# Two transformer blocks on one core: relative bias read back skewed from DRAM, and three re-orderings in the first mixer

## The chip, the cores and the metric

The kernel runs on one core of one Trainium2 chip. The metric is the device time of one execution, in microseconds. Before the change it is 933.23 us, the median of 3 runs (931.76 to 933.48).

## The reference, cut to what matters

The program computes two transformer blocks, one after the other, on 256 tokens of width 1024 in float32. Each block is a token mixer followed by a mixture of 32 experts. The change is in the mixer of the first block, and there in the attention branch:

```python
qb = rms_norm(qb.reshape(b, t, 8, 64), g_q)
kb = rms_norm(kb.reshape(b, t, 8, 64), g_k)
score = einsum('bqhs,bqh->bqs', relu(q_idx . k_idx), w_idx)   # indexer, then the top 64 keys of each query
logits = einsum('bqhd,bqkhd->bqhk', qb, k_sel) * 64 ** -0.5
bias = rel_bias[t5_bucket(key_pos - query_pos)]               # (32, 8) table, one number per head and distance
p = softmax(logits + bias)
out = einsum('bqhk,bqkhd->bqhd', p, v_sel)
```

The bias depends on the head and on key minus query position alone, so 512 numbers per head hold all of it. A tile of 128 queries needs, in partition p, the row of those numbers shifted by p: later queries see smaller distances.

## The kernel before, in words

**Weights** stream from DRAM through 5 slots of 2 MB; a load into a slot is issued from SP's queue as soon as the weight that stood there has been used up. The order of loads in the first mixer is index, keys (KB), queries (QB), values (VB), then the projections of the gated linear attention (GLA_R, GLA_QK, GLA_V), the gates, the branch and output matrices, and then the experts.

**A projection** (`project`, L314) multiplies the 256 tokens by a 1024x512 weight in 8 steps of k. For each step `split` (L268) cuts the 128x512 weight piece into two parts that TensorE takes in its fast float32r form: ACT copies the rounded value (`whi`, L279) and DVE or POOL subtracts it from the weight (`wlo`, L280). Which of the two subtracts follows from the string in `SPLIT_ENGINES` that `turn[2]` selects: 'vp' alternates between DVE and POOL. There are 4 buffers of `whi` and of `wlo`. A step is six 512-column matmuls (L285) for the two token tiles.

**The order of work.** The instructions are written in one program, and a planner in the library fixes each engine's queue when the kernel is built. It walks the program with its own cost estimates and gives an engine, at each point, the ready instruction that stands first in the program; a split is moved ahead by 30 places (`SPLIT_AHEAD`). It also gives out the buffers of a tag. The queues run in that fixed order on the chip, so an instruction that waits holds up everything behind it on its engine.

**The attention branch** of the first mixer, in program order: the index projection and its scores (L524 to L541, DVE's multiply-adds at L557 and L559, the eight rounds of MAX8 and MATCH_REPLACE8 at L564 and L565, and the mask at L567); the key projection and its norm `kn` (L570; `head_norm`, L361, with the squares at L367, the sums at L368 and the multiply at L371); the bias row; the query projection; `pairs_T` of the keys (L374: 8 transposes at L381, two evictions on DVE at L387); the norm of the queries and their `pairs_T`; the value projection; then `scores` (L409) per tile of 128 queries: the mask matmuls (L596), the score matmuls (L422), the addition of the bias on DVE (`add_rel`, L599), maximum, exponentials and `values`.

**The bias row.** A matmul of the bias table with a one-hot bucket table (L573) gives 8 heads x 512 distances; DVE copies it to `relT` (L574), a tile of the tag "sq", of which there are 2 buffers (`head_norm` uses the same tag for its squares). SP writes it to DRAM as 8 rows of 2 KB (`rel_d`, L575) and, when that has landed, reads it back twice (L578): partition p reads the 256 numbers from place p on, so rows run the wrong way round. Four groups of matmuls with an anti-diagonal matrix, `flip` (L587), turn the 128 partitions upside down, and ACT copies the result into `relB` (L589).

**Loads at the start**: SP issues the first half of `X` (L223), then the pack `zk` with the identity matrix (L216), then the second half of `X`. The first instructions of TensorE transpose `X` (L348) and need both.

Of the kernel before, what the change touches and what calls it, by code (L numbers as in the profile page):

```python
# [11 lines left out]
F32 = mybir.dt.float32  # L12
# [3 lines left out]
AF = mybir.ActivationFunctionType  # L16
# [4 lines left out]
P = 128  # L21
T = 256
NT = 2
# [3 lines left out]
CAP = 32  # L27
N_STREAM = 5
SPLIT_AHEAD = 30
SPLIT_ENGINES = ('vp', 'pv')  # L30
LAST_COLUMNS = ((0, 2), (2, 1), (3, 1))
WCOLS = 4096

# [1 line left out]
QB, KB, VB, IDX, GATE_A, GATE_B = 1552, 2064, 2576, 3088, 3384, 4408  # L35
# [36 lines left out]
def tables(a):  # L72
    z, c, m1, m2, e = (Pack() for _ in range(5))
    i = np.arange(P)
    f = np.float32

    def feat(name, shape=(8, P)):
        return a[name].reshape(shape).T

    def twice(name):  # L80
        return np.concatenate([a[name].reshape(64, 1)] * 2, 0)

    z.add("ident", np.eye(P, dtype=f))
    z.add("g_mix", feat("g_mix"))

    c.add("g_ffn", feat("g_ffn"))
    c.add("g_ffn_i", a["g_ffn"].reshape(P, 8))
    c.add("ggla", a["g_gla"].reshape(P, 1))
    c.add("n_mix", feat("norm_mix_2"))
    c.add("n_ffn", feat("norm_ffn_2"))  # L90
    c.add("n_ffn_i", a["norm_ffn_2"].reshape(P, 8))
    c.add("br1", rows(np.concatenate([a["b_rg"].ravel(), a["b_re"].ravel()])))
    c.add("br2", rows(np.concatenate([a["b_router_group_2"].ravel(), a["b_router_expert_2"].ravel()])))
    c.add("iota", rows(np.arange(CAP, dtype=f) - 4096))
    c.add("rev4", rows(f(4) - np.arange(4, dtype=f)))
    c.add("owner", ((i[:, None] // 32) == np.arange(4)[None, :]).astype(f))

    m1.add("gq", twice("g_q"))
    m1.add("gk", twice("g_k"))
    m1.add("wa2", np.concatenate([a["w_alpha2"].reshape(16, 256), a["b_alpha"].reshape(1, 256)], 0))  # L100
    m1.add("relb", a["rel_bias"].reshape(32, 8))
    same = (i[:, None] // 64) == (i[None, :] // 64)
    m1.add("after", ((i[:, None] > i[None, :]) & same).astype(f) / 16)
    m1.add("chunk", ((i[:, None] // 64) == np.arange(2)[None, :]).astype(f) / 16)
    m1.add("flip", np.eye(P, dtype=f)[::-1])

    m2.add("gqf", twice("q_norm_fox_2"))
    m2.add("gkf", twice("k_norm_fox_2"))
    c.add("gof", feat("out_norm_fox_2", (4, P)))
    m2.add("god", feat("out_norm_dil_2", (4, P)))  # L110
    m2.add("gqd", rows(a["q_norm_dil_2"]))
    m2.add("gkd", rows(a["k_norm_dil_2"]))
    m2.add("bfg", rows(a["b_forget_2"]))
    m2.add("upto", (i[:, None] <= i[None, :]).astype(f))
    inv = (f(1) / (f(10000.0) ** (np.arange(0, 64, 2, dtype=f) / f(64)))).astype(f)
    ang = np.arange(T, dtype=f)[:, None] * inv[None, :]
    for name, fn in (("cos", np.cos), ("sin", np.sin)):
        m2.add(name, fn(ang).astype(f).reshape(2, P, 32).transpose(1, 0, 2).reshape(P, 64))
    m2.add("selrow", (((i[:, None] % 32) == np.arange(8)[None, :]) & (i[:, None] < 96)).astype(f))
    d = i[:, None] + P - np.arange(T)[None, :]  # L120
    n = ((d >= 0) & (d <= 128)).astype(int) + ((d >= 0) & (d % 4 == 0)) + ((d >= 0) & (d % 16 == 0))
    m2.add("ln", np.where(n > 0, np.log(np.maximum(n, 1)), NEG).astype(f))

    rel = np.arange(512) - 255
    e.add("bucket", (t5_bucket(rel)[None, :] == np.arange(32)[:, None]).astype(f))
    e.add("before", (i[:, None] < i[None, :]).astype(f))
    e.add("causal", np.where(i[None, :] > i[:, None], f(NEG), f(0)).astype(f))
    return {"zk": z, "ck": c, "m1": m1, "m2": m2, "ek": e}
# [25 lines left out]
def two_blocks(ctx: ExitStack, tc: tile.TileContext, A: dict, at: dict, out: bass.AP):  # L154
    nc = tc.nc
# [39 lines left out]
    def bank(name="ps", bufs=4):  # L195
        return psum.tile([P, 512], F32, name=name, tag=name, bufs=bufs)
# [11 lines left out]
    def t5(shape, dt=F32):  # L208
        return wtile(shape, dt, tag="b5", bufs=2, level="misc")

    X = const.tile([P, NT, D], F32, name="X")
    packs = {}

    def load_pack(name, level="const"):
        packs[name] = wtile([P, A[name].shape[1]], tag=name, bufs=1, level=level)
        nc.sync.dma_start(packs[name], A[name])  # L216

    def con(name):
        p, o, n = at[name]
        return packs[p][:, o:o + n]  # L220

    for tt in range(NT):
        nc.sync.dma_start(X[:, tt, :], A["x"][0, tt * P:(tt + 1) * P, :])  # L223
        if tt == 0:
            load_pack("zk")

    open_phase("mix1")
    open_phase("mix1_b4", "mid")
# [37 lines left out]
    turn = [0, None, 0]  # L266
# [47 lines left out]
    def project(src, c0, ns, hT, then=None, step=8):  # L314
        ws = [wload(src, 8 * (c0 + sum(ns[:i])), 8, n, step) for i, n in enumerate(ns)]
        ac = [[acc() for _ in range(NT)] for _ in ns]
        gemm_tok(ws, hT, ac, then)
        return ac if len(ns) > 1 else ac[0]
# [42 lines left out]
    def head_norm(ps2, rstd):  # L361
        q = t4([P, NT, 512])
        ss = wtile([P, NT, 8], tag="hss", bufs=2)
        for tt in range(NT):
            sq = wtile([P, 512], tag="sq", bufs=2, level="const")
            scaled(q[:, tt, :], ps2[tt], rstd[:, tt:tt + 1])
            nc.scalar.activation(sq, q[:, tt, :], AF.Square)  # L367
            nc.vector.reduce_sum(ss[:, tt, :], sq.rearrange("p (h d) -> p h d", h=8), axis=AX.X)  # L368
        rs = rsqrt_mean(ss.rearrange("p t h -> p (t h)"), 16, 1.0 / 64)
        qv = q.rearrange("p t (h d) -> p (t h) d", d=64)  # L370
        nc.vector.tensor_mul(qv, qv, rs[:, :, None].to_broadcast([P, 16, 64]))  # L371
        return q

    def pairs_T(q, g, scale):  # L374
        dst = t4([P, 4, T])
        for j in range(2):
            ps = bank()
            for a in range(2):
                for tt in range(NT):
                    pair = 2 * j + a  # L380
                    nc.tensor.transpose(ps[:, a * T + tt * P:a * T + (tt + 1) * P],  # L381
                                        q[:, tt, pair * P:(pair + 1) * P], ident)
            d = dst[:, 2 * j:2 * j + 2, :].rearrange("p a t -> p (a t)")
            if g is None:
                nc.vector.tensor_scalar_mul(d, ps, scale)
            else:
                nc.vector.tensor_scalar(d, ps, g, scale, op0=OP.mult, op1=OP.mult)  # L387
        return dst
# [119 lines left out]
    w_in = A["w_in"]  # L508
    hT = to_feat(con("g_mix"))
# [8 lines left out]
    causal_b = const.tile([P, P], BF16, name="causal_b")  # L518
    relT = wtile([P, 512], tag="sq", bufs=2, level="const")
    dram = ctx.enter_context(tc.tile_pool(name="scratch", bufs=1, space=bass.MemoryType.DRAM))  # L520
    rel_d = dram.tile([8, 512], F32, name="rel_d")
    relB = wtile([P, 8, T], tag="relB", bufs=1, level="misc")

    a2 = [acc(), acc()]  # L524
# [1 line left out]
    rstd = r_[0]  # L526
# [3 lines left out]
    for tt in range(NT):  # L530
        r = rstd[:, tt:tt + 1]
# [4 lines left out]
    for tt in range(NT):  # L536
        ps = bank()
# [29 lines left out]
        nc.vector.tensor_scalar(mk[:, :Kn], sc[:, :Kn], -2e38, NEG, op0=OP.is_gt, op1=OP.mult)  # L567
        masks.append(mk)

    kn = head_norm(project(w_in, KB, [512], hT), rstd)  # L570

    ps = bank()
    nc.tensor.matmul(ps[:8, :], con("relb")[:32, :], con("bucket")[:32, :], start=True, stop=True)  # L573
    nc.vector.tensor_copy(relT[:8, :], ps[:8, :])  # L574
    nc.sync.dma_start(rel_d, relT[:8, :])  # L575
    relH = [t5([P, 4, T]) for _ in range(2)]
    for r in range(2):
        nc.sync.dma_start(relH[r], bass.AP(tensor=rel_d.tensor, offset=rel_d.offset + r * 512,  # L578
                                           ap=[[1, P], [1024, 4], [1, T]]))

    qp = project(w_in, QB, [512], hT)
    kTd = pairs_T(kn, con("gk"), 1.0)
    qn = head_norm(qp, rstd)
    qTd = pairs_T(qn, con("gq"), 0.125)
    for j in range(4):
        ps = bank()
        nc.tensor.matmul(ps, con("flip"), relH[j // 2][:, j % 2 * 2:j % 2 * 2 + 2, :].rearrange("p h k -> p (h k)"),  # L587
                         start=True, stop=True)
        nc.scalar.activation(relB[:, 2 * j:2 * j + 2, :].rearrange("p h k -> p (h k)"), ps, AF.Copy)  # L589

    nc.gpsimd.tensor_copy(before_b, con("before"))
    nc.gpsimd.tensor_copy(causal_b, con("causal"))

# [6 lines left out]

    vb = t4([P, NT, 512])
    a2 = project(w_in, VB, [512], hT)
    for tt in range(NT):
        scaled(vb[:, tt, :], a2[tt], rstd[:, tt:tt + 1])
    attT = [t4([P, 4, T], F32R) for _ in range(2)]
# [8 lines left out]
    for tt in range(NT):  # L614
        r = rstd[:, tt:tt + 1]
# [3 lines left out]
    ps = bank()  # L619
# [37 lines left out]
    ps = bank()  # L657
# [11 lines left out]
    for tt in range(NT):  # L669
        for h in range(4):  # L670
            pair, r = divmod(h, 2)
# [16 lines left out]
    for tt in range(NT):  # L688
        for c in range(2):
            for h in range(4):  # L690
                pair, r = divmod(h, 2)
# [30 lines left out]
    ps = bank()  # L722
# [414 lines left out]
    hT = to_feat(con("n_mix"))  # L1137
# [31 lines left out]
    kb = project(w_in2, 2048, [512], hT, (3, lambda: token_rstd(r_)), 4)  # L1169
    rstd = r_[0]  # L1170
# [9 lines left out]
    for tt in range(NT):  # L1180
        r = rstd[:, tt:tt + 1]
# [138 lines left out]
```

## Time and profile before

| what | before |
|---|---|
| median of 3 runs | 933.23 us |
| the profiled execution | 932.74 us, span 931.1 us |
| PE busy (matmul) | 748.7 us, 80% |
| DVE / ACT / POOL busy | 369.0 / 272.0 / 170.4 us |
| DMA | 304.68 MB, mean 327 GB/s |

The span runs from the first instruction to the last, on the one core. PE is TensorE, PEld its weight loads, DVE VectorE, ACT ScalarE, POOL GpSimd, SP the engine whose queue issues nearly all DMAs. A line such as L285 is that line of the kernel. "Idle before, <- X" tells what ended an engine's idle time. The granted clock of TensorE is given as a share of 2.4 GHz, so 0.5 is the lower level of 1.2 GHz.

### The profile page before, as it was taken

To read this page: it belongs to the slowest core of one execution; us is meant where nothing else is said; L and a number is where in the kernel's file an instruction comes from. 1 tells how busy PE (TensorE), PEld (TensorE's weight loads), DVE (VectorE), ACT (ScalarE), POOL (GpSimd) and SP (SyncE) were. 2 spreads that over 40 slices of the span, in tenths; PEclk is the share of its full clock that TensorE was granted. 3 is DMA by queue.
4 is the path that set the end of the run, shared out by engine and by line. 5 is a ranking of instruction groups with operands and counts; after the bars stand their busy time and mean duration, and the time that the engine had idled before them with its cause. 6 is when DMAs were issued, how large, how long until landed. Compare 5 with 4: busy or idle time off the path is not lost.

```text
span 931.1 us, 13946 instructions
## 1 busy us (share of the span) xinstructions
PE 748.7 (80%) x5662; PEld 474.7 (51%) x5662; DVE 369.0 (40%) x788; ACT 272.0 (29%) x617; POOL 170.4 (18%) x158
## 2 busy tenths in 40 slices
PE   7999999998999988898899956756575666666666
PEld 6668889986766767686774412312131122121213
DVE  4966365575554568759572301002020011010102
ACT  6456555544111165564671100000000000000000
POOL 3332344574000036423240000000000000000001
PEclk9999999999999999999999978788798798797977
DMA  9562445667599984424668999999999999999997
GB/s 365 222 232 96 177 146 216 271 272 270 225 426 424 419 345 171 187 92 168 225 248 347 429 428 427 428 428 426 426 427 427 428 428 427 429 428 427 427 419 285
DMA packets 26487, 304.68 MB, mean 327 GB/s; under 512 B 2920, under 2 KB 4712, under 8 KB 8368
## 3 DMA queue, kind: packets, MB, share of 16 engines
q1 hardware_dynamic: 25840, 302.68, 79.0%
q8 instruction: 46, 0.75, 0.3%
q0 software_dynamic: 288, 0.79, 0.2%
q10 hardware_dynamic: 288, 0.26, 0.1%
q14 instruction: 25, 0.20, 0.1%
HBM read 302.65 MB, written 1.06 MB: 326 GB/s over the span
## 4 chain that ended last, share of the span: by engine, by line
DMA 44%; PE 9%; DVE 3%; ACT 2%; issue 1%; DVEq 0%; SPq 0%; ACTq 0%
DMA w<-w_up 16%; DMA w<-w_gate 13%; DMA w<-w_down 13%; PE acc L285 4%; DMA w<-w_last 2%; PE acc L1110 2%; PE ps L459 1%; ACT b L438 1%; PE ps L1006 1%; PE ps L452 1%; ACT whi L279 0%; DVE wlo L280 0%; ACT b L359 0%; ACT H L504 0%; PE ps L422 0%
## 5 line engine op out<-in xcount | busy, mean ns | idle before, releaser
L1110 PE MATMUL acc<-w,XT 128*32 128x128 f32 (+1 forms) x2048 | 186.9, 495 | 77.6 <-DMA w<-w_up 50.9
L280 POOL TENSOR_TENSOR wlo<-w,whi 128x512 fp32r<-128x512 f32 (+3 forms) x104 | 134.1, 1294 | 193.0 <-ACT whi L279 167.3
L1110 PEld LDWEIGHTS acc<-w,XT 128*32 128x32 f32 x2048 | 58.9, 116 | 174.4 <-issue 95.6
L279 ACT ACTIVATE whi<-w 128x512 fp32r<-128x512 f32 (+3 forms) x208 | 120.0, 591 | 84.0 <-PE acc L285 73.5
L1060 PE MATMUL acc<-w,pT 128*32 128x512 f32 (+1 forms) x712 | 98.2, 671 | 51.9 <-DMA w<-w_down 48.4
L280 DVE TENSOR_TENSOR wlo<-w,whi 128x512 fp32r<-128x512 f32 (+3 forms) x104 | 80.2, 776 | 52.8 <-ACT whi L279 50.1
L1032 DVE TENSOR_TENSOR on<-acc,sq 128x512 fp32r<-128x512 f32 (+1 forms) x35 | 22.5, 645 | 179.3 <-ACT sq L1031 178.8
L285 PE MATMUL acc<-whi,aT_hi 128*128 128x512 f32 (+3 forms) x240 | 89.6, 378 | 0.9 <-ACT whi L279 0.6
L285 PE MATMUL acc<-whi,aT_lo 128*128 128x512 f32 (+3 forms) x240 | 87.7, 370 | 0.0
L1040 POOL DMA_DIRECT2D out<-X x6 | 3.4, 574 | 432.7 <-DVE X L1038 432.7
L1060 PEld LDWEIGHTS acc<-w,pT 128*32 128x32 f32 x712 | 23.5, 123 | 115.3 <-DMA w<-w_down 62.3
L285 PE MATMUL acc<-wlo,aT_hi 128*128 128x512 f32 (+3 forms) x240 | 70.5, 374 | 6.5 <-POOL wlo L280 3.5
L1031 ACT ACTIVATE sq<-acc 128x512 fp32r<-128x512 f32 (+1 forms) x35 | 19.5, 561 | 165.2 <-PE acc L1060 165.2
L1044 DVE SCALAR_TENSOR_TENSOR on<-acc,sc,sq 128x128 f32<-128x128 f32 (+1 forms) x16 | 11.6, 723 | 129.6 <-PE acc L1110 128.6
L1054 ACT ACTIVATE pT<-ps 128x128 f32<-128x128 f32 (+1 forms) x16 | 7.0, 437 | 184.8 <-PE ps L1052 158.7
L285 PEld LDWEIGHTS acc<-whi,aT_hi 128*128 128x128 f32 x240 | 47.3, 197 | 10.3 <-issue 1.5
L285 PEld LDWEIGHTS acc<-wlo,aT_hi 128*128 128x128 f32 x240 | 44.0, 198 | 14.9 <-DVE wlo L280 4.2
L285 PEld LDWEIGHTS acc<-whi,aT_lo 128*128 128x128 f32 x240 | 47.3, 197 | 7.0 <-issue 0.9
L1021 ACT ACTIVATE ST<-ps 128x256 fp32r<-128x256 f32 x16 | 6.1, 383 | 138.3 <-PE ps L1018 138.3
L1038 DVE TENSOR_TENSOR X<-X,ps 128x512 f32<-128x512 f32 (+1 forms) x70 | 40.5, 636 | 5.0 <-PE ps L1036 4.7
L1006 PE MATMUL ps<-S,H 128*128 128x128 f32 x256 | 36.0, 298 | 3.4 <-PEq L923 3.4
L1006 PEld LDWEIGHTS ps<-S,H 128*128 128x128 f32 x256 | 33.1, 208 | 9.9 <-issue 8.3
(277 smaller groups left out, 1085.3 us busy)
## 6 DMA issues: line engine op xcount, KB each, us to landing
w<-w_up SPq DMA_DIRECT2D x40, 2048.0 KB, 39.1
w<-w_gate SPq DMA_DIRECT2D x40, 2048.0 KB, 39.1
w<-w_down SPq DMA_DIRECT2D x35, 2048.0 KB, 39.1
w<-w_in SPq DMA_DIRECT2D x13, 2048.0 KB, 9.8
w<-w_last SPq DMA_DIRECT2D x18, 512.0 KB, 12.5
w<-w_out SPq DMA_DIRECT2D x4, 2048.0 KB, 7.3
w<-w_in SPq DMA_DIRECT2D x2, 1056.0 KB, 18.9
w<-w_in SPq DMA_DIRECT2D x2, 1040.0 KB, 13.3
```

The costliest lines, as they stand in the source:

```text
L279: turn[1] = nc.scalar.activation(r[0], v, AF.Copy)
L280: eng.tensor_sub(r[1], v, r[0].bitcast(F32))
L285: nc.tensor.matmul(out_, a, b, start=start, stop=stop, **kw)
L438: nc.scalar.activation(prob[:, r, s], src, AF.Exp, bias=bias[:, 2 * s + r:2 * s + r + 1], accum_out=sm[:, h:h + 1])
L452: nc.tensor.transpose(ps[:, q * P:(q + 1) * P], prob[:, r, s, tok(kt)], ident)
L1006: nc.tensor.matmul(ps[:, kk * n:(kk + 1) * n], h[:, tt, kp + kk, :], S[:, tt].rearrange("p e s -> p (e s)"), start=i == 0, stop=i == len(t ...
L1031: nc.scalar.activation(yh, yp[:, :n], AF.Copy)
L1032: nc.vector.tensor_sub(yl, yp[:, :n], yh.bitcast(F32))
L1038: nc.vector.tensor_add(xs, xs, ps[:, :n])
L1044: nc.vector.scalar_tensor_tensor(hid.rearrange("s c p -> s p c"), gu[1][:, :F].rearrange("s (p c) -> s p c", c=n2), sc[:, 1:2], sg[:, :F]. ...
L1060: nc.tensor.matmul(yp[js], hT_[:, c, js], w, start=c == 0, stop=c == n2 - 1)
L1110: mm = nc.tensor.matmul(gu[i][32 * j:32 * j + 32, :F], XT[k * gn // 8][:, k % (8 // gn), (g % gn) * P + 32 * j:(g % gn) * P + 32 * j + 32] ...
```

## The change

The strings of `SPLIT_ENGINES` get a third, 'pp', which the key projection alone uses: all its eight subtractions go to POOL. The `flip` matrix, its matmuls and ACT's copies are gone. Instead the DMA to DRAM writes each of the 8 rows of `relT` 128 times, into a buffer of 8 x 128 x 512 numbers (2 MB where it was 16 KB), and the two reads take, for partition p, the 256 numbers from place 127 - p of copy p, straight into `relB`. The transposes of keys and queries are written behind the value projection. The pack with the identity is issued first on SP, the first half of `X` on ACT's queue and the second on SP's.

```diff
-SPLIT_ENGINES = ('vp', 'pv')
+SPLIT_ENGINES = ('vp', 'pv', 'pp')
...
-    m1.add("flip", np.eye(P, dtype=f)[::-1])
...
-    for tt in range(NT):
-        nc.sync.dma_start(X[:, tt, :], A["x"][0, tt * P:(tt + 1) * P, :])
-        if tt == 0:
-            load_pack("zk")
+    load_pack("zk")
+    for tt, eng in enumerate((nc.scalar, nc.sync)):
+        eng.dma_start(X[:, tt, :], A["x"][0, tt * P:(tt + 1) * P, :])
...
-    rel_d = dram.tile([8, 512], F32, name="rel_d")
+    rel_d = dram.tile([8, P, 512], F32, name="rel_d")
...
-    kn = head_norm(project(w_in, KB, [512], hT), rstd)
+    turn[2] = 2
+    kb = project(w_in, KB, [512], hT)
+    turn[2] = 0
+    kn = head_norm(kb, rstd)
...
-    nc.sync.dma_start(rel_d, relT[:8, :])
-    relH = [t5([P, 4, T]) for _ in range(2)]
+    nc.sync.dma_start(rel_d, relT[:8, None, :].to_broadcast([8, P, 512]))
     for r in range(2):
-        nc.sync.dma_start(relH[r], bass.AP(tensor=rel_d.tensor, offset=rel_d.offset + r * 512,
-                                           ap=[[1, P], [1024, 4], [1, T]]))
+        nc.sync.dma_start(relB[:, 4 * r:4 * r + 4, :],
+                          bass.AP(tensor=rel_d.tensor, offset=rel_d.offset + r * P * 512 + P - 1,
+                                  ap=[[511, P], [2 * P * 512, 4], [1, T]]))
 
     qp = project(w_in, QB, [512], hT)
-    kTd = pairs_T(kn, con("gk"), 1.0)
     qn = head_norm(qp, rstd)
-    qTd = pairs_T(qn, con("gq"), 0.125)
-    for j in range(4):
-        ps = bank()
-        nc.tensor.matmul(ps, con("flip"), relH[j // 2][:, j % 2 * 2:j % 2 * 2 + 2, :].rearrange("p h k -> p (h k)"),
-                         start=True, stop=True)
-        nc.scalar.activation(relB[:, 2 * j:2 * j + 2, :].rearrange("p h k -> p (h k)"), ps, AF.Copy)
...
     a2 = project(w_in, VB, [512], hT)
+    kTd = pairs_T(kn, con("gk"), 1.0)
+    qTd = pairs_T(qn, con("gq"), 0.125)
```

## Rows read from the trace of the kernel before

**Rows 1.** The page: its first line, and PE's and the DMAs' busy tenths in 40 slices.
```profile
span 931.1 us, 13946 instructions
...
PE   7999999998999988898899956756575666666666
...
DMA  9562445667599984424668999999999999999997
```
**Rows 2.** The chain that ended last: its first piece, and where DMAs take over.
```profile
380.03 2.89 PE acc L285 x12
...
517.43 31.57 DMA w<-w_up
```
**Rows 3.** Windows: stretch, length, busy PE, PEld, DVE, ACT, POOL, PEclk, DMA share, GB/s.
```profile
24.00:39.00 15.00, 13.07 (x48) 9.38 (x46) 14.59 (x47) 6.67 (x13) 5.14 (x4) 0.89 0.62 239
...
50.00:53.00 3.00, 1.12 (x9) 0.79 (x8) 3.00 (x5) 2.74 (x5) 0.72 (x1) 1.00 0.84 262
...
60.00:63.05 3.05, 3.05 (x10) 1.37 (x9) 1.97 (x3) 1.45 (x3) 0.11 (x1) 1.00 0.61 172
...
517.00:931.00 414.00, 269.76 (x1794) 94.62 (x1786) 54.92 (x125) 21.57 (x39) 3.43 (x6) 0.84 0.99 419
```
**Rows 4.** Timeline of PE: start, us, line, operation, tiles, shape, idle before.
```profile
33.21 0.73 PE L285 MATMUL acc<-wlo,aT_hi 128*128 128x512 f32 x2 [1.93 <-DVE wlo L280]
...
52.24 1.06 PE L381 MATMUL ps<-zk,b 128*128 128x128 f32 x8 [1.88 <-DVE b L371]
...
69.05 1.16 PE L422 MATMUL ps<-b,b 64*128 64x128 f32 x16
```
**Rows 5.** Timeline of DVE.
```profile
28.09 1.48 DVE L559 SCALAR_TENSOR_TENSOR score<-b,wi,score 128x256 f32<-128x256 f32 x1
...
29.76 0.47 DVE L559 SCALAR_TENSOR_TENSOR score<-b,wi,score 128x256 f32<-128x256 f32 x1
...
44.84 0.67 DVE L574 COPY sq<-ps 8x512 f32<-8x512 f32 x1
...
60.58 1.40 DVE L387 TENSOR_SCALAR b<-ps,m 128x512 f32<-128x512 f32 x2
...
68.76 0.43 DVE L280 TENSOR_TENSOR wlo<-w,whi 128x264 fp32r<-128x264 f32 x1 [2.30 <-ACT whi L279]
70.24 1.29 DVE L599 TENSOR_TENSOR b<-ps,relB 128x512 f32<-128x512 f32 x2 [1.05 <-PE ps L422]
```
**Rows 6.** Timeline of POOL.
```profile
28.00 1.29 POOL L280 TENSOR_TENSOR wlo<-w,whi 128x512 fp32r<-128x512 f32 x1 [1.09 <-ACT whi L279]
```
**Rows 7.** Timeline of ACT.
```profile
51.59 1.15 ACT L367 ACTIVATE sq<-b 128x512 f32<-128x512 f32 x2
```
**Rows 8.** Timeline of SP's queue: DMA issues.
```profile
1.30 0.42 SPq L216 DMA_DIRECT2D zk<-zk  x1
1.77 0.42 SPq L223 DMA_DIRECT2D X<-x  x1
```
**Rows 9.** The DMA view, 35 to 45 us: one 2 MB weight load.
```profile
DMA packets 144, 2.10 MB, mean 210 GB/s; under 512 B 16, under 2 KB 16, under 8 KB 16
```
**Rows 10.** The DMA view, 45.9 to 47 us: the write of rel_d.
```profile
DMA packets 16, 0.02 MB, mean 15 GB/s; under 512 B 8, under 2 KB 8, under 8 KB 16
...
q1 hardware_dynamic: 16, 0.02, 8.0%
```
**Rows 11.** Its packets that start in 46.326 to 46.336, and in 46.47 to 46.6 us.
```profile
q1 hardware_dynamic: 1, 0.00, 157.5%
...
q1 hardware_dynamic: 6, 0.00, 9.5%
```
**Rows 12.** The DMA view, issues: KB each, median us to landing; packets of 56 to 61 us.
```profile
b<-rel_d SPq DMA_DIRECT2D x2, 512.0 KB, 10.0
...
DMA packets 1217, 1.21 MB, mean 243 GB/s; under 512 B 64, under 2 KB 1216, under 8 KB 1216
```
**Rows 13.** Windows of the matmuls of L285 alone, 70.14 to 74.3 us (GLA_R's projection).
```profile
70.14:74.30 4.16, 3.88 (x30) 3.67 (x30) 1.00 0.00 0
```

## Prediction

> **What bounds the kernel now.** I read the page first. The span is 931.1 us [rows 1], the profiled execution 932.74 us, so 1.64 us lie around the span; it is 0.49 us under the median of 933.23, and I add that at the end. About 0.2% (1.9 us) is what a measurement of this kernel can tell from no change. Next the chain that ended last: it begins with the second mixer's matmuls at 380 us and from 517 us on is a row of weight transfers [rows 2], in a stretch where the DMAs are busy 0.99 of the time at 419 GB/s [rows 3]. So the end is set by transfers, and they start when weight slots come free, which the mixers' own progress decides. The chain doesn't reach back to the first 100 us, so for these I read the slices of 23.3 us: from the second to the seventh, to 163 us, PE stands at 9 tenths or more, while the DMAs stand at 2 to 6 [rows 1]. Nothing there is held by transfers, and the work behind waits for PE. I take it that what the first mixer gains or loses moves the end by as much.
>
> Between 24 and 63 us two engines bound it together. DVE is busy 14.59 of 15 us to 39, and 3.00 of 3 from 50 [rows 3], and PE stops twice for it: 1.93 us for a key split, 1.88 us for the normed keys [rows 4]. The clock granted from 24 to 39 us averages 0.89 [rows 3]: after the first stop part of the stretch ran at 1.2 GHz, and 0.11 of 15 us, 1.65 us, is its price.
>
> **The change part by part.** Loads at the start: SP issues one DMA fewer ahead of the second half of X, so that moves up by 1.77 - 1.30 = 0.47 us, as does zk [rows 8]. ACT's issue and its table load come before ACT has input. Worth -0.47 (0 to -0.5).
>
> Flips: their matmuls hold PE from 60.0 to 63.05, where it is busy throughout [rows 3]: -3.05 us. ACT's four copies and the flip columns ran beside other work: 0.
>
> Transposes behind the values: PE no longer stops for the normed keys, -1.88 [rows 4]. But the evictions now end on the path: one of 0.70 us (two take 1.40 [rows 5]) stands between the last transpose and the scores, +0.7. That cover was the flips.
>
> Key splits on POOL: DVE loses four two-input operations of 0.65 us each (two 128x512 ones take 1.29 [rows 5]), 2.6 us. Against it stands a row: the multiply-add at 28.09 took 1.48 us while POOL's split ran from 28.00 to 29.29, and the same operation took 0.47 at 29.76 [rows 5, 6]. A split on POOL holds such a DVE operation for up to 1.0 us, so four more cost up to 4.0. On DVE the edit is worth -2.6 to +1.4. PE could gain the stop and the slow clock, 1.93 + 1.65 = 3.6 us; but it would then reach the query splits earlier, and half of those stay on a DVE that is no earlier. I take 0 (-3.6 to +1.4).
>
> Those parts sum to -0.47 - 3.05 - 1.88 + 0.7 = -4.7 us: the scores of 69.05 [rows 4] would begin near 64.8, and their bias be wanted 1.2 us later as now [rows 4, 5], near 66.0. DVE allows it: its last eviction ends at 61.98 [rows 5].
>
> **The write to DRAM** is the costly part. Now 8 rows of 2 KB move; 16 packets, 8 of them the small completions [rows 10]. A 2 MB load shows 16 completions [rows 9], so I read the write as running on half the DMA engines, one row each. The change makes it 8 x 128 rows from the same 8 partitions: 128 rows for each of eight engines. Price of one row: two that start when the others are nearly through share, with four completions, 9.5% of 16 engines in 0.13 us, so 0.1 us each; one that starts among the others takes 157.5% of 16 engines in 0.01 us, 0.252 us [rows 11]. That is 128 x 0.1 = 13 us at least on eight engines, or 5 us if the new shape spreads over all (2 MB at 419 GB/s [rows 3]). At most the whole round, some 0.33 us from 46.32 to 46.65, is paid 128 times: 43 us. I take 0.252, for in a long write each row has company: W = 32.3 us. By the Trainium skill this is worse: "DMA: Bandwidth & Descriptors", Rules for kernel authors, says that an outermost dimension under 16 confines a DMA to as many engines, and "SBUF — State Buffer", Door 1, that bandwidth follows the ports that the partitions reach, 27.2 GB/s each. Partitions 0 to 7 reach two, which would make W an estimated 38.5 us and the total 953.6.
>
> When is relB there? DVE's copy of the row ends at 45.5 and packets start at 46.3 [rows 5, 11]. DVE gains and loses about as much before it, so I leave it there. Then W; 1 us for completion and issue; then the reads. Now they take 10.0 us to landing, with a weight load ahead, and their 1 KB packets move in the last 5 [rows 12]. I take 7 (5 to 10). So relB is there at 46.3 + W + 8 = 54.3 + W = 86.6 us, 20 us after it is wanted.
>
> Who waits: SP, for the write, before the reads and whatever load is queued behind; those weights are wanted late, 0. DVE, at the first addition of the bias, and behind that in its queue GLA_R's splits. Two of those stand ahead of it in the profile, the second at 68.76 [rows 5], so PE gets two steps of 12 matmuls done, at 4.16/30 = 0.139 us each 3.3 us [rows 13], and then stops too. It restarts after a long stop; I charge the 1.65 us that the short one cost.
>
> Sum: the addition moves from 70.24 to 86.6, +16.4; work done ahead -3.3; clock +1.65; start -0.47. That is +14.2 us, or in general W - 18.1. Against 932.74 it is 946.9, on the median's scale 947.4. W is 22.5 by the mean of the eight rows (8.0% of 16 engines in 1.1 us [rows 10], 0.176 us each) and 43 by the round: 937.6 to 958.1.
>
> **Rivals.** (a) The write is hidden: W is 11.7 us or less, so relB is there by 66.0. For it: a row alone takes 0.1, and W is 13 then, near enough; eight engines may get their rows without hindering each other. Against: the row of 0.252. Time: 932.74 - 4.7 + 0.49 = 928.5 (925 to 930 with the key splits' bounds). It decides below W = 11.7, and up to W = 18.1 the gain is merely eaten. The build's planner could also reach it by queueing the scores later; a planner that expects the write to be short has no cause to.
>
> (b) All eight rows hinder one another, as the round of 0.33 us would have it: W from 36 to 43, 951 to 958. The two pages of the Trainium skill named above lead here too.
>
> (c) The write keeps relT's buffer, one of two that the squares of the query norm take at 51.59 [rows 7]. If the planner gave them that buffer, ACT stops there until the write is read out, and the last value splits wait behind it. The scores then come some 8 us after the write (the values' last four steps and the transposes), 46.3 + 32.3 + 8 = 86.6, but with no GLA_R done ahead: 950.7.
>
> (d) W near 18: no difference that can be measured.
>
> **How the numbers follow.** Forecast 0.38 (W from 20 to 36), (b) 0.18, (c) 0.06, (d) 0.05, (a) 0.33. Slower is 0.38 + 0.18 + 0.06 = 0.62, the same 0.05, faster 0.33. The likeliest case has its own range, 938 to 952; with (a) as a third of the chance, the range must take in both sides, 926 to 957. The likeliest time is 947.4.
>
> **What would show it.** DVE idle before its first bias addition, ended by a DMA from rel_d, with PE idle beside it and before it 1024 packets of 2 KB at 50 to 90 GB/s; the flips' 3 us and the stop before the key transposes gone; long DVE multiply-adds beside POOL's splits. It is wrong if the write's packets end before 58 us, or if PE has other work queued in the wait.

## The result and the profile after

The changed kernel takes 944.9 us (median of four executions, 944.01 to 947.62) against 933.36 us for the kernel before on the same chip: a ratio of 1.0132 with a 95% interval of 1.0109 to 1.0154, so it is slower by 1.3%. The profiled execution is the longest of the four, 947.62 us with a span of 945.9 us; line numbers of the changed kernel stand 2 to 7 under those of the kernel before.

The page after: its first line, and PE's and the DMAs' busy tenths in 40 slices.

```profile
span 945.9 us, 13929 instructions
...
PE   7898898999898988898899975756566566575666
...
DMA  9554944368499995342658999999999999999997
```

The chain that ended last, after (start, us, what), where the transfers take over:

```profile
532.45 31.34 DMA w<-w_up
```

The transfers take over at 532.45 us instead of 517.43 [rows 2]: the 15 us are lost ahead of the second mixer's end, and nothing behind gives them back. PE's slices show where: the second, fourth, fifth and seventh, all ahead of 166 us, have fallen from 9 tenths to 8 [rows 1]. Two wide windows (columns as in [rows 3]) put most of it on one stretch. The kernel before:

```profile
24.00:90.00 66.00, 60.92 (x340) 48.50 (x339) 52.26 (x124) 35.64 (x87) 21.23 (x19) 0.97 0.45 169
90.00:180.00 90.00, 89.51 (x689) 83.37 (x689) 46.01 (x75) 53.09 (x96) 40.04 (x30) 1.00 0.51 201
```

The changed kernel:

```profile
24.00:90.00 66.00, 59.71 (x315) 49.18 (x315) 48.14 (x110) 32.19 (x65) 27.15 (x23) 0.95 0.49 117
90.00:180.00 90.00, 80.30 (x595) 72.14 (x594) 44.71 (x78) 46.58 (x100) 29.00 (x21) 0.92 0.53 214
```

From 90 to 180 us PE is busy 80.30 us instead of 89.51, at a granted clock of 0.92 instead of 1.00. PE's timeline after gives the single stops and the places that answer to [rows 4]:

```profile
41.39 1.22 PE L283 MATMUL acc<-wlo,aT_hi 128*128 128x512 f32 x2 [4.66 <-DVE wlo L278]
...
53.78 0.74 PE L283 MATMUL acc<-wlo,aT_hi 128*128 128x512 f32 x2 [1.41 <-DVE wlo L278]
...
68.25 1.18 PE L420 MATMUL ps<-b,b 64*128 64x128 f32 x16
...
80.37 0.40 PE L283 MATMUL acc<-wlo,aT_hi 128*128 128x264 f32 x2
...
98.46 0.80 PE L283 MATMUL acc<-whi,aT_hi 128*128 128x512 f32 x1 [6.29 <-ACT whi L277]
...
152.96 1.22 PE L283 MATMUL acc<-aT_hi,wlo 128*128 128x256 f32 x4 [3.18 <-DVE wlo L278]
```

The key projection no longer stops, nor do the key transposes. In their place the query projection stops twice for a DVE split, 4.66 and 1.41 us, so the scores start only 0.8 us earlier (68.25 against 69.05). Then comes a change nobody wrote: GLA_R's last step (128x264) is done at 80.37 us, where in the kernel before the bias addition at 70.24 [rows 5] runs in the midst of it. At 98.46 us PE has stood 6.29 us. SP's queue after tells why:

```profile
48.21 0.86 SPq L576 DMA_DIRECT2D rel_d<-sq  x1
53.80 0.66 SPq L260 DMA_DIRECT2D w<-w_in  x1
92.75 0.94 SPq L578 DMA_DIRECT2D relB<-rel_d  x2
93.80 1.69 SPq L260 DMA_DIRECT2D w<-w_in  x3
```

The DMA view after, 45 to 75 us, issues (KB each, us to landing):

```profile
w<-w_in SPq DMA_DIRECT2D x1, 2048.0 KB, 43.9
```

GLA_V's weights, issued at 53.80 behind the write, need 43.9 us where four 2 MB loads took 7.9 in the median before; ACT splits them at 97.78. And the write itself, from the DMA view of 64 to 88 us:

```profile
DMA packets 578, 1.20 MB, mean 50 GB/s; under 512 B 0, under 2 KB 0, under 8 KB 576
## 3 DMA queue, kind: packets, MB, share of 16 engines
q1 hardware_dynamic: 576, 1.18, 44.9%
```

576 rows in 24 us on eight engines is one row per engine every 0.333 us, of which 0.449 x 16 x 24 / 576 = 0.299 us is the packet itself. 128 of them make W = 42.7 us. SP cannot issue the reads before 92.75, and relB is there near 100. DVE's timeline:

```profile
98.96 1.36 DVE L278 TENSOR_TENSOR wlo<-w,whi 128x512 fp32r<-128x512 f32 x1 [11.29 <-ACT whi L277]
100.24 0.68 DVE L592 TENSOR_TENSOR b<-ps,relB 128x512 f32<-128x512 f32 x1
```

The first bias addition is 30.0 us later than in [rows 5]. Between 70 and 100 us PE has done GLA_R and GLA_QK ahead of it, which in the kernel before came behind it. So three things can be the cause: late data (weights and bias), the order of work that goes with the long write, and the key splits.

### The profile page after: what moved, and what is told of

Read it like the earlier page. It is cut to its first block, busy times and chain, and to the rows that moved or that the text cites. A ratio compares the mean times of both kernels' runs of the same rounds, so it can differ in the third digit from the quotient of the medians.

```text
span 945.9 us, 13929 instructions
## 1 busy us (share of the span) xinstructions
PE 751.8 (79%) x5654; PEld 476.5 (50%) x5654; DVE 368.8 (39%) x784; ACT 270.1 (29%) x613; POOL 175.1 (19%) x162
## 4 chain that ended last, share of the span: by engine, by line
DMA 43%; PE 17%; DVE 3%; ACT 3%; issue 1%; POOL 1%; DVEq 0%; ACTq 0%; SPq 0%; POOLq 0%
DMA w<-w_up 16%; DMA w<-w_gate 13%; DMA w<-w_down 12%; PE acc L283 6%; PE acc L1105 3%; DMA w<-w_last 2%; PE ps L1001 2%; PE ps L1031 1%; PE ps L457 1%; PE acc L1055 1%; POOL sq L1158 1%; ACT b L436 1%; ACT whi L277 1%; PE ps L450 1%; DVE wlo L278 0%
## 5 line engine op out<-in xcount | busy, mean ns | idle before, releaser
L278 POOL TENSOR_TENSOR wlo<-w,whi 128x512 fp32r<-128x512 f32 (+3 forms) x108 | 138.7, 1291 | 206.0 <-ACT whi L277 186.7
L278 DVE TENSOR_TENSOR wlo<-w,whi 128x512 fp32r<-128x512 f32 (+3 forms) x100 | 76.7, 772 | 62.5 <-ACT whi L277 57.6
L1055 PEld LDWEIGHTS acc<-w,pT 128*32 128x32 f32 x712 | 23.7, 123 | 115.6 <-DMA w<-w_down 59.6
L283 PE MATMUL acc<-wlo,aT_hi 128*128 128x512 f32 (+3 forms) x240 | 73.2, 384 | 10.9 <-DVE wlo L278 7.1
L1004 DVE TENSOR_TENSOR XT<-ps,ck 128x256 f32<-128x256 f32 (+1 forms) x48 | 24.6, 512 | 33.0 <-PE ps L1001 32.9
## 6 DMA issues: line engine op xcount, KB each, us to landing
w<-w_in SPq DMA_DIRECT2D x13, 2048.0 KB, 11.3
w<-w_last SPq DMA_DIRECT2D x18, 512.0 KB, 11.5
```

The costliest lines, as they stand in the source:

```text
L278: eng.tensor_sub(r[1], v, r[0].bitcast(F32))
L283: nc.tensor.matmul(out_, a, b, start=start, stop=stop, **kw)
L1004: nc.vector.tensor_mul(XT[kp * gn // 8][:, k:k + 2, :], ps[:, :2 * n].rearrange("p (k s) -> p k s", k=2), gI[:, kp:kp + 2, None].to_broadc ...
L1055: nc.tensor.matmul(yp[js], hT_[:, c, js], w, start=c == 0, stop=c == n2 - 1)
```

## The experiments

Each was timed in five rounds beside the kernel before; ratios are to that kernel, with the 95% interval. Theory A is the one I began with.

**The four edits taken apart.** One run takes the skewed read out of the changed kernel (the diff), one puts it alone into the kernel before (the same lines the other way).

```
-    nc.sync.dma_start(rel_d, relT[:8, None, :].to_broadcast([8, P, 512]))
+    nc.sync.dma_start(rel_d, relT[:8, :])
...
+        nc.tensor.matmul(ps, con("flip"), relH[j // 2][:, j % 2 * 2:j % 2 * 2 + 2, :].rearrange("p h k -> p (h k)"),
+                         start=True, stop=True)
```

> The changed kernel with the skewed read undone (16 KB write, rows in mirror order, four flip products); key splits on POOL, transposes behind the value projection and identity first stay. Theory A (the 2 MB write stands ahead of GLA_V's weights in the rings of eight DMA engines; that is the slowdown): GLA_V's load lands within 10 us of its issue instead of 43.9, TensorE has no stop over 2 us near 98 us, time 931 to 936 us. Theory B (the key splits on POOL alone: they move the stop into the query projection, 4.66 and 1.41 us, and cost the clock): the query stops stay and the time is 939 to 945 us.

Measured: 933.16 us, 1.001 (0.9985 to 1.0035). GLA_V's load lands after 8.7 us, and the stop in the query projection is there, larger than in the changed kernel. PE's timeline of this run:

```profile
41.53 1.22 PE L284 MATMUL acc<-wlo,aT_hi 128*128 128x512 f32 x2 [5.62 <-DVE wlo L279]
```

Without the long write the slowdown is gone, and the other three edits together are worth nothing that can be measured.

> The kernel before with the skewed read alone; the other three edits left out. Theory A: the write runs some 42 us at about 50 GB/s, the 2 MB weight load issued behind it takes over 35 us, time 940 to 948 us. Theory B: the flips and the wait on the eviction of the keys are gone and little takes their place, time 929 to 936 us.

Measured: 941.01 us, 1.0085 (1.0063 to 1.0106); the load behind the write lands after 45.9 us. As theory A had it.

**The key splits shared again**, the rest of the change kept:

```
-    turn[2] = 2
     kb = project(w_in, KB, [512], hT)
-    turn[2] = 0
```

> The changed kernel with the key splits shared between DVE and POOL again; the narrow 2 MB write stays. Theory A: GLA_V's load still lands over 35 us after its issue, TensorE still stops there, time 942 to 949 us. Theory B: the query stops of 4.66 and 1.41 us go, a stop of some 1.9 us in the key projection comes back, time 934 to 940 us.

Measured: 941.48 us, 1.0097 (1.0074 to 1.0119), between the two ranges. The write still does most of the harm, but the key splits on POOL alone add 0.35%, 3.3 us (from two comparisons of 0.2% uncertainty each, so only just clear of the noise). This run has the stop back in the key projection and none in the query's, and its scores start at 63.92, 4.3 us ahead of the changed kernel's. Its PE timeline:

```profile
33.12 1.22 PE L283 MATMUL acc<-wlo,aT_hi 128*128 128x512 f32 x2 [3.25 <-DVE wlo L278]
...
63.92 1.18 PE L420 MATMUL ps<-b,b 64*128 64x128 f32 x16
```

What DVE pays is in its groups by shape, 18 to 50 us (count | busy us, mean ns | idle before). The changed kernel:

```profile
L557 DVE SCALAR_TENSOR_TENSOR score<-b,wi,score 128x128 f32<-128x128 f32 x7 | 4.4, 632 | 0.5
...
L559 DVE TENSOR_SCALAR score<-score 64x64 f32<-64x64 f32 x2 | 2.3, 1154 | 0.0
```

This run:

```profile
L557 DVE SCALAR_TENSOR_TENSOR score<-b,wi,score 128x128 f32<-128x128 f32 x7 | 2.5, 352 | 0.5
...
L559 DVE TENSOR_SCALAR score<-score 64x64 f32<-64x64 f32 x2 | 0.4, 185 | 0.0
```

With all key splits on POOL the same seven multiply-adds take 632 ns each instead of 352, and two small 64x64 operations 1154 instead of 185. In the kernel before they take 492 and 172. Both long 64x64 operations, at 27.69 and 36.53 us, ran beside splits on POOL (26.22 to 31.37 and 36.35 to 37.62); those of this run, at 24.82 and 32.29, did not.

**The write from 128 partitions.** Each head's row is made in 16 partitions, and each partition writes 8 copies; the bytes in DRAM and the read stay.

```
-    m1.add("relb", a["rel_bias"].reshape(32, 8))
+    m1.add("relb", np.repeat(a["rel_bias"].reshape(32, 8), 16, axis=1))
...
-    nc.sync.dma_start(rel_d, relT[:8, None, :].to_broadcast([8, P, 512]))
+    nc.sync.dma_start(rel_d.rearrange("h (c j) k -> (h c) j k", c=16), relT[:, None, :].to_broadcast([P, 8, 512]))
```

> The changed kernel, the same 2 MB written from 128 partitions (each head's row stands in 16 of them, 8 copies from each) instead of from 8. Theory A: the write takes 6 to 12 us on 16 engines, GLA_V's load lands within 12 us, relB is there before the scores (68 us), time 928 to 935 us. Theory B: the query stops of 4.66 and 1.41 us stay, time 939 to 945 us. If the bytes themselves were what hurts, and not the eight engines, the time stays at 945 too, with the query stops no cause.

Measured: 929.65 us, 0.9972 (0.9956 to 0.9988): faster than both. The query stop of 5.07 us is there, so theory B falls as the main cause. The DMA view of this run, 48 to 54 us:

```profile
DMA packets 1007, 2.06 MB, mean 344 GB/s; under 512 B 0, under 2 KB 0, under 8 KB 1007
## 3 DMA queue, kind: packets, MB, share of 16 engines
q1 hardware_dynamic: 1007, 2.06, 93.6%
```

A row now costs 0.936 x 16 x 6 / 1007 = 0.089 us, and 2 MB are through in 6 us. With the key splits shared as well (this diff and the one before it):

> The changed kernel with the write from 128 partitions and the key splits shared between DVE and POOL again (two parts undone or altered; the read, the transposes behind the value projection and identity first stay). Theory A: the narrow write was the loss and the key splits on POOL alone a second, smaller one (3.4 us between the changed kernel and the run with shared key splits), so 925 to 928 us. If the key splits cost only beside the narrow write, it stays at 929 to 931 us.

Measured: 928.02 us, 0.9948 (0.9929 to 0.9967), the best version of all, at the upper edge of theory A's range, its scores starting at 64.96 us. It is 2.2 us under the run above; with these intervals that difference is likely and not certain. The wide write and the skewed read alone, on the kernel before:

> The kernel before with the skewed read alone, from a write out of 128 partitions; transposes, key splits and the order of the first loads as before. Theory A: faster than the kernel before by the flips and the wait they brought, 2 to 5 us, so 927 to 930 us. If the transposes behind the value projection carry part of the gain, the run with them (wide write, shared keys) is faster than this one by 1 to 3 us; if they and identity first are worth nothing, the two agree within 1 us.

Measured: 929.59 us, 0.9974 (0.9952 to 0.9995). The transposes behind the values and the identity first seem worth the 2.4 us between the two, with the same reserve.

**Which part of the long write hurts?** First, does GLA_V's load wait because it stands behind the write in the same queue? The write alone moves to ScalarE's queue.

```
-    nc.sync.dma_start(rel_d, relT[:8, None, :].to_broadcast([8, P, 512]))
+    nc.scalar.dma_start(rel_d, relT[:8, None, :].to_broadcast([8, P, 512]))
```

> The changed kernel with the narrow 2 MB write issued from ScalarE's queue instead of SyncE's, so that it stands in rings of its own and not ahead of GLA_V's weights; the reads stay on SyncE's queue behind it. Theory A1 (order within one ring): GLA_V's load shares the eight engines with the write and lands in 14 to 25 us instead of 43.9, TensorE does not stop for it, the write itself takes 45 to 52 us, time 933 to 941 us. Theory A2 (the eight engines take the write as a whole first, whichever queue it is in): GLA_V's load still lands after 40 us, 943 to 948 us.

Measured: 966.09 us, 1.0363 (1.0334 to 1.0391). The load lands after 22.3 us instead of 43.9, as A1 says, but the time is a miss: something else stood. ACT's timeline of this run:

```profile
48.05 1.29 ACTq L576 DMA_DIRECT2D rel_d<-sq  x1
...
93.70 0.63 ACT L365 ACTIVATE sq<-b 128x512 f32<-128x512 f32 x1 [33.07 <-DMA rel_d<-sq]
```

The squares of the query norm have got the buffer that the write is still reading, and ACT stands 33 us for it: rival (c) of the prediction, in a kernel where the changed one escaped it. Next the write stays on SyncE's queue but is made to wait for GLA_V's issue:

```
...
+    ahead = [wload(w_in, 8 * c, 8, n) for c, n in ((VB, 512), (GLA_R, 264), (GLA_R + 264, 264), (GLA_QK, 512), (GLA_V, 512))]
+    with tc.issue_after(turn[3].ins):
+        nc.sync.dma_start(rel_d, relT[:8, None, :].to_broadcast([8, P, 512]))
```

> The changed kernel with the narrow 2 MB write made to wait in SyncE's queue until GLA_V's load has been issued (the gate weights that follow are issued behind the write, and the reads behind those). Theory A1 (order within one ring): GLA_V's load lands within 12 us, TensorE's stop of 6.3 us near 98 us for it is gone; the gate load now lands after 35 to 45 us and relB at 105 to 112 us, so a stop comes later, at the bias or the gates: time 936 to 946 us. Theory C (the late bias, not the late weights, makes the loss): the bias is some 6 us later still, so the time is 948 to 954 us.

Measured: 951.49 us, 1.0198 (1.0166 to 1.0231). GLA_V lands after 8.4 us and PE does not stop for it, yet against the kernel before the time is 0.66% worse than the changed kernel's. The gate weights now stand behind the write (42.1 us to landing), and the bias is added from 108.61. Its PE timeline:

```profile
106.83 0.58 PE L284 MATMUL acc<-aT_hi,whi 128*128 128x256 f32 x1 [4.00 <-ACT whi L278]
```

So GLA_V's weights were not the loss by themselves: whatever is late next takes their place. That is theory C's number, but not its proof: the bias is 8.4 us later than in the changed kernel, and the order of work is another one too (the matmul at 106.83 is the first of the gates, which in the changed kernel come at 123.97). In the next run the write goes out on ScalarE's queue from a buffer of its own, GLA_V's load ahead of the reads, and the blocks GLA_R and GLA_QK are written ahead of the scores.

```
-    relT = wtile([P, 512], tag="sq", bufs=2, level="const")
+    relT = wtile([P, 512], tag="relT", bufs=1, level="misc")
...
+    nc.scalar.dma_start(rel_d, relT[:8, None, :].to_broadcast([8, P, 512]))
...
+    with tc.issue_after(turn[3].ins):
+        for r in range(2):
+            nc.sync.dma_start(relB[:, 4 * r:4 * r + 4, :],
...
     a2 = project(w_in, GLA_QK, [512], hT, ws=ahead[3:4])
...
+    attT = [t4([P, 4, T], F32R) for _ in range(2)]
+    for tt in range(NT):
+        on = values(scores(tt, qTd, kTd, add_sel, add_rel, neg_max), vb)
```

> The changed kernel with the narrow write issued from ScalarE's queue and out of a buffer of its own (so that nobody waits for that buffer), GLA_V's load issued ahead of the reads, and the blocks GLA_R and GLA_QK written ahead of the scores, which keeps the order of TensorE's work near that of the changed kernel. GLA_V's weights then come in time (landing 15 to 25 us after issue, near 77 us) while relB comes as late as in the changed kernel (98 to 101 us). Theory A (the late weights of GLA_V make the loss): TensorE has no stop for weights, 930 to 936 us. Theory C (the late bias makes it; the weights only share the delay): the stop moves to the products behind the first bias addition, 939 to 946 us.

Measured: 934.59 us, 1.0021 (1.0006 to 1.0036), though the write is as slow as before. The order came out other than I had said: the scores themselves start only at 95.30 us, relB lands near 95, and its first addition follows at once. PE's timeline of this run:

```profile
95.30 1.16 PE L421 MATMUL ps<-b,b 64*128 64x128 f32 x16
```

Its DVE timeline:

```profile
96.49 1.29 DVE L595 TENSOR_TENSOR b<-ps,relB 128x512 f32<-128x512 f32 x2
```

From 90 to 180 us PE is busy 87.81 of 90 us. The time is in theory A's range, but with another order the run does not part A from C. A slow write is nearly free where the order of work asks for its result late.

**Late data or the order?** The write from 16 partitions halves W and leaves the order alone.

```
+    nc.tensor.matmul(ps[:16, :], con("relb")[:32, :], con("bucket")[:32, :], start=True, stop=True)
...
+    nc.sync.dma_start(rel_d.rearrange("h (c j) k -> (h c) j k", c=2), relT[:16, None, :].to_broadcast([16, 64, 512]))
```

> The changed kernel with the same 2 MB written from 16 partitions (each head's row in two, 64 copies from each). If the number of partitions sets the rate of the write, it takes half as long, some 21 us instead of 42.6, so relB is there near 78 us; by the prediction's own rule (shift = W - 18.1 us) that is 3 us over the kernel before: 934 to 938 us. If the write had been slow for its bytes or for its 2 KB rows, it stays near 42 us and the time at 945.

Measured: 939.63 us, 1.0078 (1.0055 to 1.0101). W halves (98 GB/s, 23.7 us from issue to landing), but the time is above the range. By its list of waits no instruction of an engine waits for a DMA from 45 to 185 us, relB is there near 79 us, and still its first addition comes at 93.34. Up to the scores this run and the one with 128 partitions agree within 0.01 us (66.54 and 66.55). Then they part. From 20 us to the experts the traces show one and the same order of work on PE, DVE, ACT and POOL in the changed kernel, in this run and in the next one with eight spread partitions, and another order with 128. Two lines of PE's timeline are marks, the last step of GLA_R and the first matmul of the first block's experts (`S,H_hi`). With 16 partitions:

```profile
78.58 0.40 PE L283 MATMUL acc<-wlo,aT_hi 128*128 128x264 f32 x2
...
238.71 0.36 PE L1001 MATMUL ps<-S,H_hi 128*128 128x256 f32 x1
```

With 128 partitions:

```profile
91.33 0.41 PE L283 MATMUL acc<-wlo,aT_hi 128*128 128x264 f32 x2
...
230.72 0.36 PE L1001 MATMUL ps<-S,H_hi 128*128 128x256 f32 x1
```

With 16 partitions GLA_R runs in one piece ahead of the values, as in the changed kernel; with 128 it is spread between them. The first order reaches the experts 8.0 us later. Windows from the scores to that mark (columns as in [rows 3]), with 16 partitions and with 128:

```profile
66.54:238.71 172.17, 160.88 (x1149) 142.01 (x1149) 93.07 (x172) 91.53 (x192) 76.77 (x61) 0.99 0.59 229
...
66.55:230.72 164.17, 158.31 (x1149) 141.17 (x1149) 94.28 (x172) 90.71 (x192) 76.43 (x61) 1.00 0.54 212
```

Both do 1149 matmuls there. With 16 partitions PE stands still for 11.3 us instead of 5.9, and is busy 2.6 us longer at a lower granted clock. What the first order lacks is cover: PE stops for ACT's exponentials and for a late split, which the changed kernel has too, at 152.96. PE's timeline with 16 partitions:

```profile
97.83 0.33 PE L450 MATMUL ps<-zk,b 128*128 128x128 f32 x1 [2.11 <-ACT b L436]
...
146.08 0.74 PE L283 MATMUL acc<-aT_hi,wlo 128*128 128x256 f32 x4 [3.18 <-DVE wlo L278]
```

To have a short write in that order, and to see what makes a row slow, the eight rows were put into partitions 0, 4, 8 to 28:

```
+    nc.vector.tensor_copy(relT[:32, :], ps[:32, :])
+    nc.sync.dma_start(rel_d, relT[0:32:4, None, :].to_broadcast([8, P, 512]))
```

> The changed kernel with the eight rows in partitions 0, 4, 8 to 28 instead of 0 to 7, still 128 copies from each of eight partitions (zero columns stand between the heads' columns of the bias weights). Theory P (the two places of the SBUF that partitions 0 to 7 share set the price of a row; the Trainium skill, SBUF - State Buffer, Door 1, gives these eight partitions eight ports instead of two): a row costs 0.1 us instead of 0.33, the write takes 13 to 16 us. Theory E (a row out of one partition repeated, or eight engines, costs 0.33 us wherever it lies): the write stays at 42 to 44 us and the time at 943 to 947 us. If P holds, the time tells of the order of work: theory D (the order that was laid out for a long write costs 7 us whether the data are late or not, as in the run with 16 partitions) says 938 to 941 us; if the late data were the whole loss, 929 to 934 us.

Measured: 937.94 us, 1.0055 (1.0035 to 1.0076). The DMA view of this run, 50 to 52 us:

```profile
q1 hardware_dynamic: 200, 0.41, 52.5%
```

200 rows in 2 us, 0.525 x 16 x 2 / 200 = 0.084 us each, 205 GB/s from eight partitions: theory P, though from the issue of the write to that of the reads only 12.7 us pass (46.82 to 59.55), under its 13 to 16. SP issues the reads at 59.55 us, the data are 26 us ahead of the first addition at 93.61, and the time is still 0.55% over the kernel before: theory D, 0.1 us under its range. The order alone costs 0.0055 + 0.0028 = 0.83%, 7.7 us, against the wide write; the late data cost the rest of the changed kernel's loss, 0.0132 - 0.0055 = 0.77%, 7.2 us. Each of these can be some 2.5 us more or less, and how the late data's share divides between the bias and GLA_V's weights stays open. That the build laid out this order because it took a write from few partitions to be long is argued, not shown; the code of the runs with 8, 16 and 128 partitions differs in nothing else than how the row is made and written.

## Why the prediction was right, and where it was not

The forecast was slower, 947.4 us with 938 to 952 for the likeliest case, and 944.9 came. That a write whose price is in its rows makes the bias late was right. The rest was in part luck. The W that came, 42.7 us, belongs to rival (b), 951 to 958, and by the prediction's own rule (W - 18.1) would have cost 24.6 us; the time stayed in the likeliest case because errors cancel.

- **W** was mis-sized: 32.3 us forecast, 42.7 measured. The step that failed is the choice of the packet's own 0.252 us [rows 11] as the row's price "for in a long write each row has company". The price was the whole round of 0.333 us, which stood there as the upper end, 43 us. The reason was another one too. What slows a row is not that several engines run at once (from 16 partitions, with the engines busy 91% of the time from 52 to 70 us, a row costs the same 0.333), but the place that it is read from (0.084 from partitions 0, 4 to 28). Here the page that spoke against the change was nearer than my row: the Trainium skill, "SBUF — State Buffer", Door 1, gives 27.2 GB/s a port, an estimated 54 for two. Measured were 50.
- **relB's arrival** was forecast at 86.6 us and came near 100: 10.4 us from W, and 2.7 from DVE's copy of the row, which I left where it was and which moved from 44.84 [rows 5] to 47.51, pushed by the key splits (with these shared it stands at 42.44). The 7 us for the reads were right (7.0).
- **The work done ahead** was forecast at 3.3 us, two steps of GLA_R. PE did all of GLA_R and GLA_QK. What came of it shows at the first matmul of the experts. PE's timeline, before and after:

```profile
234.01 0.78 PE L1006 MATMUL ps<-S,H_hi 128*128 128x256 f32 x1
...
246.51 0.36 PE L1001 MATMUL ps<-S,H_hi 128*128 128x256 f32 x1
```

The windows from the scores to it, before and after:

```profile
69.05:234.01 164.96, 159.12 (x1155) 141.87 (x1153) 94.76 (x175) 91.92 (x194) 76.38 (x61) 1.00 0.52 205
...
68.25:246.51 178.26, 164.23 (x1150) 145.05 (x1149) 92.87 (x172) 91.76 (x192) 76.51 (x61) 0.96 0.60 220
```

Of the 30.0 us by which the addition was late 12.5 remained. That "PE has other work queued in the wait" stood among what would make the prediction wrong. It had, and yet the shift came near the forecast (+14.2; +11.5 by the medians), because too short a W and too little work ahead offset each other. The changed order has a price of its own besides, 7.7 us by the runs above, which stood nowhere in the sum.

- **Who waits** was wrong: those weights "are wanted late, 0". GLA_V's load got issued right behind the write and was PE's stop of 6.29 us. DVE never waited for rel_d at the addition, which was the sign I had named: it stood 11.29 us for the split of those weights, and the addition followed at once.
- **The clock** cost more than 1.65 us. In the windows above PE is busy 5.1 us longer with nearly the same matmuls, and the granted clock fell to 0.58 from 98.5 to 105 us, behind the stop of 6.29 us, and to 0.50, the lower level, from 153 to 158, behind that of 3.18.
- **Key splits**: -2.6 to +1.4 us was the bound for DVE, PE taken as 0. Measured, +3.3 us in the changed kernel, above it, though with an uncertainty that reaches back into it. The row of 1.48 us [rows 5] was the right row; what I missed is that a split on the other engine is dearer still where DVE's operation is short (1154 ns instead of 185 for 64x64), and that the stop only moves on into the query projection, larger. Without that edit the scores start at 63.92 and 64.96; my 64.8 was a good forecast for a kernel without it.
- **Flips, normed keys, start** (-4.7 us upstream): right in size. Rival (a), the hidden write at 928.5 us with 925 to 930, is the kernel with the wide write, 0.9972 to 0.9948, which is 930.7 to 928.5 us on the scale of 933.36.

## What to carry to other kernels

A DMA's price is set by where in the SBUF it reads as much as by its bytes (here 42.7 us or 6 us for the same 2 MB): copy a small row into many partitions, or spread a few partitions apart, before writing it out many times. A long transfer costs more than its own wait: whatever is issued behind it on the same engines comes late, and a changed order of work that came with it keeps costing when the transfer is short again. And an engine that hands work to another may still lose by it, as DVE did beside POOL; ask where the stop goes next.

## What was not expected of the hardware

- The rate of a write of 2 KB rows: 50 GB/s from partitions 0 to 7, 98 from 0 to 15, 205 from 0, 4 to 28, 344 from all 128. At 50 and at 205 there are eight partitions, and about half of the engines' time is taken (44.9% and 52.5%), so neither the number of partitions nor that of the engines is the bound at 50. It agrees with the page of the Trainium skill named above, by which these are two, four, eight and sixteen ports: the first three rates are some 25 GB/s a port, a little under the page's 27.2. At 344 GB/s the engines themselves are busy 93.6% of the time.
- Order within one queue: 2 MB of weights behind the write landed after 43.9 us, in a queue beside it after 22.3 us, ahead of it after 8.4 us. In the last case the write was issued 0.38 us later and hardly slowed the load.
